# A hybrid delta-rule and pooling layer: the chunk inverse in 16-bit pairs, and the order of the work around it

## The chip, the cores and the metric

The kernel runs on one core of a Trainium2 chip, in one launch. A core has a matrix engine (TensorE, PE in the profile; its weight loads are PEld), three engines for elementwise work (VectorE is DVE, ScalarE is ACT, GpSimd is POOL) and SyncE (SP), which here issues the DMAs. The metric is the device time of one execution in microseconds; times of kernels are medians of several runs.

## The reference

One layer over 2048 new frames of one stream and 64 of a running one, model width 1024, all in float32. A norm and one combined input projection feed two groups: a gated delta rule (4 heads of 128, evaluated in chunks) and a pooling group (four trailing means with a linear map each). Both go through one output projection; then follow a norm, a SwiGLU layer of inner width 2816 and a last norm. The part that matters here is the chunk's inverse T of a unit lower triangular matrix:

```python
q, k, v = causal_conv_silu(...)               # q, k l2-normalised per head
G = cumsum(g)                                 # log decay, per head and chunk
gamma = exp(where(lower_incl, G[:, None] - G[None, :], -inf))
Lm = where(lower_strict, (k * beta) @ k.T * gamma, 0)
T = inverse(eye + Lm)                         # unit lower triangular
u, w = T @ (v * beta), T @ (k * beta * exp(G))
for each chunk, with the state S:
    v_new = u - w @ S
    o = (q * exp(G)) @ S + ((q @ k.T) * gamma) @ v_new
    S = S * exp(G_last) + (k * exp(G_last - G)).T @ v_new
x = x + concat(rmsnorm(o) * silu(z), pool) @ w_out
h = rmsnorm(x)
x = x + (silu(h @ w_gate) * (h @ w_up)) @ w_down
```

The kernel takes chunks of 128 frames rather than the reference's 64, which gives the same result. The projection, a product with the state and the outputs stay in float32 or in pairs that carry about its precision.

## The kernel before

**Two phases.** The first (to about 985 us in the profile) goes through four blocks of 512 frames, the first with the 64 frames of the running stream besides. A block has a norm (`norm_stats`, `norm_apply`), 21 projection tiles of 128 columns (`project`, products `pp`): one for the gates, four for each head (`head_project`) and four for pooling (`pools`), and later eight tiles of output projection (`out_proj`, products `pz`). The second phase goes over three blocks of 704 frames: 22 gate and up tiles (`gate_up`, products `px`, `py`, `pz`), and the down projection in six groups of inner tiles.

**Dense products.** Every float32 operand of a dense product is split into a high and a low half of a reduced format (`split`, `wsplit`), and three products stand for one; these are the type "r" of the scheduler. Gate, up and most down groups use Strassen's scheme (7 products instead of 8, `down_strassen`, `factors`, `prep_down`); the groups listed in `PLAIN` are done without it (`down`, products `d`).

**The inverse.** Each head of each block has two `Front`s of two chunks each, 32 in all, and the running stream has one. A front makes the decay matrix (gb: the row of G by `rowmm`, minus G by `negmm` with `seln`, a mask by `idbf` with `negm`, then one exponential into Gam), the matrix U (Gst) and then its inverse by doubling, in six steps after a first one: POOL masks U (Um), PE multiplies (py), ACT evicts to f16 (Yt), PE multiplies (pt), DVE updates T and its transpose V, all 2 x 2 x 128 columns (TV). The last step writes float32; then two corrections in full float32 (type "f" of the scheduler, two records each in the profile) take away the error of f16: F = 1 - T - U T (pf), and X = V + F (V + F V) (two products px), each evicted by DVE. Behind the inverse a chain goes through the chunks (pk, po, Sp).

**What sets the order.** No engine is programmed by hand: `Machine` records all operations and issues each engine's in an order that a list scheduler gives, from estimated costs (`Machine.cost`; for DVE 0.15 + 1.045e-3 x elements, in us) and a rank, the place in the program minus `machine.boost`. Chains of the inverse are boosted by `BOOST`. On PE, f16 and float32 products go ahead of dense ones, once the last of them has been ready for `HOLD[0]` us or so (`Machine.pick`). The order is then fixed, and semaphores keep what is needed.

**Buffers that matter.** PSUM tiles of the dense products come from a ring of `PSM` = 3 (pc, the product of the decay rows Rt, takes one of these). `evict` empties a projection; in block 0 it is DVE that does so, and multiplies by the norm's factor rn. `bp` holds h, as two tiles of four of the eight 128-row parts each (h0 and h1), one buffer each. `new_o(last_prev, bp, None, 1)` puts the operand op of block 2's output projection into those same buffers, when block 3 has projected; `out_proj` uses op's second tile (op1, parts 4 to 7) first. The loads for it (od) go through a ring of three (xc). In the second phase the loads of h (`load_h`, xh and xhT) go through f2's ring "t" of seven from its start on, which the gates' evictions use as well.

Of the kernel before, what the change touches and what calls it, by code (L numbers as in the profile page):

```python
# [9 lines left out]
F16 = mybir.dt.float16  # L10
# [8 lines left out]
P = 128  # L19
D = 1024  # L20
# [27 lines left out]
PLAIN = ((0, 0), (0, 1), (0, 2), (0, 3), (0, 5), (1, 2), (2, 2))  # L48
# [10 lines left out]
class Machine:  # L59
# [294 lines left out]
def hybrid_kernel(ctx, tc, a, o):  # L354
# [131 lines left out]
    for j in range(NBLK):  # L486
# [4 lines left out]
        else:  # L491
            plan += win[:9] + win[17:] + win[9:17]
# [40 lines left out]
    def prep():  # L533
# [8 lines left out]
        elif key[0] in ("win", "wout"):  # L542
            parts = []
            for i in range(2):
                raw, t = (f() for f in wtiles(f"p{i}"))
                src = a[key[0]][key[1]][:, 512 * i : 512 * i + 512]
                nc.sync.dma_start(out=raw, in_=wpd[key[1]] if key[0] == "wout" and i else src)
                if key == ("win", 0):

                    r3, h3, l3 = (x.rearrange("p (k c) -> p k c", c=P) for x in (raw, t[:, 0], t[:, 1]))  # L550
                    nc.gpsimd.memset(l3[:, :, 64:].bitcast(F32), 0.0)
                    nc.scalar.copy(l3[:, :, :64], r3[:, :, :64])
                    nc.scalar.copy(h3[:, :, :64], r3[:, :, :64])
                    tt(h3[:, :, 64:], r3[:, :, 64:], l3[:, :, :64].bitcast(F32), ALU.subtract)
                else:
                    wsplit(t, raw)
# [197 lines left out]
    def norm_apply(B):  # L754
# [62 lines left out]
    nc.sync.dma_start(out=consts, in_=a["consts"])  # L817
# [22 lines left out]
    lm_f = gp.tile([P, 2, 512], F32, tag="Yqk", name="lm_f", bufs=NY).rearrange("p i (l n) -> p (i l) n", n=P)  # L840
    nc.sync.dma_start(out=lm_f, in_=a["lmask"])
    lmask = cp1.tile([P, 7, P], F16, tag="lmask", name="lmask")
    nc.vector.tensor_copy(lmask, lm_f[:, :7])
    negm = cp1.tile([P, P], BF16, tag="negm", name="negm")
    nc.vector.tensor_copy(negm, lm_f[:, 7])

    negm2 = cp1.tile([P, P], BF16, tag="negm2", name="negm2")
    nc.vector.tensor_copy(negm2, lm_f[:, 7])
    nc.vector.memset(negm2[:DEC, DEC:], -1e30)
    id16 = cp1.tile([P, P], F16, tag="id16", name="id16")  # L850
    nc.vector.tensor_copy(id16, ident)
    idbf = cp1.tile([P, P], BF16, tag="idbf", name="idbf")
    nc.vector.tensor_copy(idbf, ident)

# [5 lines left out]
    nc.vector.memset(Sp, 0.0)  # L860

# [6 lines left out]
    class Front:  # L868
# [39 lines left out]
        def negmm(self, ps):  # L908

            G = self.B.Ghl  # L910
            if self.h is None:
                for h in range(NH):
                    mm(ps[:, h * DEC : (h + 1) * DEC], G[:, SO : SO + P], seln[:, h, :].to_broadcast([P, DEC]),
                       start=False, stop=False)
            else:
                for c in range(2):
                    at = self.off + c * C
                    mm(ps[:, c * C : (c + 1) * C], G[:, at : at + C], seln[:, self.h, :].to_broadcast([P, C]),
                       start=False, stop=c == 1, skip_group_check=True)

        def all(self):
# [22 lines left out]
            TV32 = lev(F32, "TV32", "", [P, 2, 2, C])  # L944
            gb = self.ps(f"gb_{tag}")
            self.rowmm(gb, True)
            EG = TV32[:, 0]
# [6 lines left out]
            dd = gb if self.h is not None else self.ps(f"dd_{tag}")  # L954
# [832 lines left out]
```

## Time and profile before

| | |
|---|---|
| median of 3 runs | 2384.84 us (2381.84 to 2387.46) |
| profiled execution, its own time | 2383.12 us |
| its span | 2380.5 us |
| mean granted TensorE clock | 0.997 |
| two record forms of the inverse, py and pt in f16 | 448 and 768 records |
| DMA moved over the span | 540.57 MB |

The span reaches from the first to the last instruction; 2.6 us lie around it. Nearly all instructions carry line 278, that of the recorder, so groups are told apart by their tiles: `pp<-h,wsp` is a projection, `px<-hA,ws` a gate product, `pz` an output projection where it reads op and a gate product where it reads hB. `_p` marks the heads of the prompt, `_s` the running stream. A row of a group gives its operations, their busy time and the mean ns of one, and behind the second bar the engine's idle time ahead of them with what ended it.

### The profile page before, as it was taken

The page shows a single profiled execution, that of the slowest core. Times are in us where ns is not written, and L with a number is a line of the kernel's source. Part 1 is how long each engine was busy: PE and PEld are TensorE (multiplying, and loading weights), DVE is VectorE, ACT ScalarE, POOL GpSimd, SP SyncE. Part 2 cuts the span into 40 slices and gives each one's busy share as a digit, 9 for nine tenths or more (in the row PEclk, how much of TensorE's full clock was granted, in tenths as well). Part 3 has the DMA queues.
Part 4 walks back from the last instruction along what each step waited for, and adds up shares of the span by engine and source line. Part 5 has one row for each costly group of instructions (what it writes and reads, how often), then busy time and mean ns, then how long its engine had stood idle before and what let it go on. Part 6 is the DMA issues. An engine that isn't in the chain of part 4 may idle for free.

```text
span 2380.5 us, 41651 instructions
## 1 busy us (share of the span) xinstructions
PE 2344.3 (98%) x14823; PEld 2184.7 (92%) x14823; DVE 1674.3 (70%) x2943; ACT 1215.7 (51%) x2738; POOL 967.2 (41%) x1130
## 2 busy tenths in 40 slices
PE   9999999999999999999999999999999999999998
PEld 8999798777887778899999999999999999999998
DVE  7999875785577686787776883767566657646466
ACT  6666654564456565574454654553334554425334
POOL 1656452554346662264332536353233464202211
PEclk9999999999999999999999999999999999999999
DMA  7643566445555565998876678887855697565763
GB/s 267 224 165 134 189 228 217 146 165 190 176 182 172 162 195 166 311 373 324 312 282 240 257 270 271 295 287 248 283 189 175 201 348 247 193 227 193 260 209 114
DMA packets 228384, 540.57 MB, mean 227 GB/s; under 512 B 28240, under 2 KB 86608, under 8 KB 228176
## 3 DMA queue, kind: packets, MB, share of 16 engines
q1 hardware_dynamic: 228176, 537.92, 66.2%
q8 instruction: 116, 1.90, 0.3%
q14 instruction: 92, 0.75, 0.1%
HBM read 389.41 MB, written 148.41 MB: 226 GB/s over the span
## 4 chain that ended last, share of the span: by engine, by line
PE 81%; DVE 9%; ACT 3%; DMA 3%; issue 2%; SPq 1%; POOL 1%; DVEq 0%; POOLq 0%; ACTq 0%
PE px L278 19%; PE pp L278 14%; PE pz L278 11%; PE py L278 9%; PE d L278 8%; PE dx L278 5%; PE dy L278 3%; PE pk_p L278 2%; PE pt_p L278 1%; PE dz L278 1%; PE gr_p L278 1%; PE px_p L278 1%; DVE Yqk L278 1%; PE py_p L278 1%; ACT E L278 1%
## 5 line engine op out<-in xcount | busy, mean ns | idle before, releaser
L278 PE MATMUL pp<-h,wsp 128*128 128x512 f32 (+1 forms) x2480 | 562.1, 366 | 2.0 <-DVE h L278 1.7
L278 PEld LDWEIGHTS pp<-h,wsp 128*128 128x128 f32 x2480 | 402.3, 190 | 49.8 <-DVE h L278 2.6
L278 POOL TENSOR_TENSOR Um_p<-Gst_p,lmask 128x256 f16<-128x256 f32 x224 | 178.2, 809 | 109.6 <-PE py_p L278 80.9
L278 PE MATMUL pz<-op,wsp 128*128 128x512 f32 (+1 forms) x960 | 216.8, 366 | 3.4 <-ACT op L278 2.9
L278 PE MATMUL d<-h3l,wsd 128*128 128x352 f32 x1248 | 201.3, 322 | 0.2 <-DVE h3l L278 0.2
L278 PEld LDWEIGHTS d<-h3l,wsd 128*128 128x128 f32 x1248 | 199.1, 188 | 1.2 <-DVE h3l L278 0.7
L278 PEld LDWEIGHTS pz<-op,wsp 128*128 128x128 f32 x960 | 155.9, 190 | 23.2 <-ACT op L278 3.4
L278 DVE TENSOR_TENSOR TV_p<-TV_p,pt_p 128x512 f16<-128x512 f16 (+1 forms) x192 | 128.5, 681 | 48.7 <-PE pt_p L278 43.4
L278 PE MATMUL px<-hA,ws 128*128 128x352 f32 x792 | 141.2, 322 | 0.6 <-DMA ws<-g 0.6
L278 PE MATMUL pz<-hB,ws 128*128 128x352 f32 x792 | 139.6, 322 | 0.6 <-DMA ws<-g 0.6
L278 PE MATMUL px<-hBT,ws 128*128 128x352 f32 x792 | 137.8, 322 | 2.1 <-DVE u L278 2.1
L278 PE MATMUL px<-hBT,wsS 128*128 128x352 f32 x792 | 137.7, 322 | 2.0 <-ACT g L278 1.9
L278 PE MATMUL py<-hB,wsS 128*128 128x352 f32 x792 | 139.2, 322 | 0.1
L278 PE MATMUL px<-hA,wsS 128*128 128x352 f32 x792 | 137.4, 322 | 0.9 <-ACT g L278 0.9
L278 PE MATMUL py<-hA,wsS 128*128 128x352 f32 x792 | 137.1, 322 | 0.0
L278 ACT ACTIVATE hr<-g 128x352 f32<-128x352 f32 x132 | 65.6, 497 | 133.4 <-DVE g L278 133.4
L278 PEld LDWEIGHTS px<-hBT,wsS 128*128 128x128 f32 x792 | 128.2, 188 | 2.8 <-ACT g L278 2.8
L278 PEld LDWEIGHTS px<-hBT,ws 128*128 128x128 f32 x792 | 128.0, 188 | 2.9 <-DVE u L278 2.7
L278 PEld LDWEIGHTS px<-hA,ws 128*128 128x128 f32 x792 | 128.9, 188 | 1.0 <-DMA ws<-g 0.9
L278 PEld LDWEIGHTS pz<-hB,ws 128*128 128x128 f32 x792 | 128.6, 188 | 0.8 <-ACT hB L278 0.8
L278 PEld LDWEIGHTS px<-hA,wsS 128*128 128x128 f32 x792 | 128.3, 188 | 1.2 <-ACT g L278 1.1
L278 PEld LDWEIGHTS py<-hB,wsS 128*128 128x128 f32 x792 | 128.6, 188 | 0.4 <-ACT u L278 0.4
(686 smaller groups left out, 5354.5 us busy)
## 6 DMA issues: line engine op xcount, KB each, us to landing
wsS<-gS SPq DMA_DIRECT2D x176, 512.0 KB, 4.7
ws<-g SPq DMA_DIRECT2D x132, 512.0 KB, 4.6
wsp<-wnd SPq DMA_DIRECT2D x126, 512.0 KB, 3.3
gS<-wsS SPq DMA_DIRECT2D x88, 512.0 KB, 5.6
g<-ws SPq DMA_DIRECT2D x66, 512.0 KB, 5.5
wnd<-wsp SPq DMA_DIRECT2D x42, 512.0 KB, 4.5
xd<-x2d SPq DMA_DIRECT2D x96, 176.0 KB, 4.0
wrd<-in_wd_dram SPq DMA_DIRECT2D x48, 256.0 KB, 4.7
```

The source lines that it names most:

```text
L278: getattr(getattr(self.nc, op.eng), name)(*args, **kw)
```

## The change

- `Front.all`: the inverse stays in f16 to its end. The update of a step writes only the half of T and V that the step can alter (`fresh`, an access pattern of runs of 2, 4, ... 64 elements), in place. U is kept as a pair of f16 halves scaled by `FS` = 256 (Uhl), and so is F (Fhl). F0 = 1 - T comes from POOL in f16, pf takes four f16 products, and the two px become one accumulation: Fhl's high half with V (evicted as FV), then its low half with V, T with 256 x identity, and Fhl's high half with FV.
- The decay matrix: `negmm` goes for the heads of the prompt; each chunk's exponential takes minus G as a bias (NG, one more small activation in `rows`).
- `Machine.pick` prefers, among the f16 and float32 products that are ready, the kind that was issued last; `HOLD[0]` is 0.6 instead of 0.4.
- `PLAIN` loses (0, 3): that down group uses Strassen's scheme now.
- The last block's pool tiles stand behind its four heads, not behind two, with h0 and h1 swapped in `new_o`.
- `norm_apply` from block 1 on: POOL multiplies by the norm's factor, ACT applies the weight as it splits, DVE makes the low half.
- `evict` ranks its operation ahead by `HURRY` = 400.
- The start: the gates' weights come in one load of 256 KB instead of two, and the first head's weights are prepared halfway through `norm_apply`; 104 of the 1384 columns of constants come early, the others and the masks behind `rows`; 19 products warm PE up instead of 22.
- `load_h` uses wpool's ring "xs" of four in all cases.

```diff
-PLAIN = ((0, 0), (0, 1), (0, 2), (0, 3), (0, 5), (1, 2), (2, 2))
+PLAIN = ((0, 0), (0, 1), (0, 2), (0, 5), (1, 2), (2, 2))
...
-            first = others[0]
+            first = min(others, key=lambda x: ((x[2].kind == "f") != (self.last == "f"), x))
...
-            plan += win[:9] + win[17:] + win[9:17]
+            plan += win
...
                     t = src(k, lo, n)
-                    stt(t, t, w, B.r[:, sl], ALU.mult, ALU.mult)
-                    split(h, sl, t)
-                if B.j == lo == 0 and k == 3:
+                    nc.gpsimd.tensor_tensor(out=t, in0=t, in1=B.r[:, sl], op=ALU.mult)
+                    act(h[:, 0, sl], t, AF.Copy, scale=w)
+                    stt(h[:, 1, sl], t, w, h[:, 0, sl].bitcast(F32), ALU.mult, ALU.subtract)
+                if B.j == lo == 0 and k % 4 == 3:
...
     def evict(B, dst, pp, p, b, n):
 
+        was, machine.boost = machine.boost, HURRY
...
+        machine.boost = was
...
-    nc.sync.dma_start(out=consts, in_=a["consts"])
+    nc.sync.dma_start(out=consts[:, :SOON], in_=a["consts"][:, :SOON])
...
+    def fresh(t, s):
+
+        (row, n), _ = t.ap
+        return bass.AP(t.tensor, t.offset, [[row, n], [2 * C + s, 2], [2 * s, 2 * C // (2 * s)], [1, s]])
...
+                mm(gb[:, : 2 * C], idbf, bc(negm, 2, C), start=False, stop=True, skip_group_check=True)
+                for c in range(2):
+                    act(Gam[:, c], two(gb)[:, c], AF.Exp, bias=self.B.NG[:, self.c0 + c, self.h : self.h + 1])
...
-                    tt(new, TV, pt.rearrange("p (t c n) -> p t c n", t=2, n=C), ALU.subtract)
-                TV = new
+                    new = fresh(TV.rearrange("p t c n -> p (t c n)"), 1 << l)
+                    tt(new, new, fresh(pt, 1 << l), ALU.subtract)
+                if l == 2:
+                    Uhl = lev(F16, "Uhl", "", [P, 2, 2, C])
+                    act(Uhl[:, 0], U, AF.Copy, scale=FS)
+                    stt(Uhl[:, 1], U, FS, Uhl[:, 0], ALU.mult, ALU.subtract)
...
-                mm(pf[:, c * C : (c + 1) * C], U[:, c], T[:, c], start=True, stop=True)
-            tt(F, F, two(pf), ALU.subtract)
+                for i in range(2):
+                    mm(pf[:, c * C : (c + 1) * C], Uhl[:, i, c], T[:, c], start=i == 0, stop=i == 1)
+            F = lev(F32, "F")
+            stt(F, F0, FS, two(pf), ALU.mult, ALU.subtract)
+            Fhl = lev(F16, "Fhl", "", [P, 2, 2, C])
+            nc.scalar.copy(Fhl[:, 0], F)
+            tt(Fhl[:, 1], F, Fhl[:, 0], ALU.subtract)
...
-                mm(px[:, c * C : (c + 1) * C], F[:, c], V[:, c], start=True, stop=True)
-            tt(T, V, two(px), ALU.add)
+                mm(px[:, c * C : (c + 1) * C], Fhl[:, 0, c], V[:, c], start=c == 0, stop=True, skip_group_check=c > 0)
+            FV = lev(F16, "Yt", "g")
+            act(FV, two(px), AF.Copy, scale=1.0 / FS)
...
-                mm(px[:, c * C : (c + 1) * C], F[:, c], T[:, c], start=True, stop=True)
-            tt(X, V, two(px), ALU.add)
+                for i, (lhsT, rhs) in enumerate(((Fhl[:, 1, c], V[:, c]), (T[:, c], idfs), (Fhl[:, 0, c], FV[:, c]))):
+                    mm(px[:, c * C : (c + 1) * C], lhsT, rhs, start=False, stop=i == 2, skip_group_check=True)
+            act(X, two(px), AF.Copy, scale=1.0 / FS)
...
-        four = [(pool or opool).tile([P, 4, 2, MB], F32R, tag=tag or f"h{k}", name=f"op{k}_{B.j}", bufs=bufs) for k in range(2)]
+        four = [(pool or opool).tile([P, 4, 2, MB], F32R, tag=tag or f"h{1 - k}", name=f"op{k}_{B.j}", bufs=bufs) for k in range(2)]
...
-            if h == 1 and nxt is None:
+            if h == NH - 1 and nxt is None:
                 pools(B)
...
-                if "pool" in wq:
-                    raw = wq["pool"].tile([P, N2], F32, tag="t", name=f"xh{nm}{k}_{b}", bufs=TB)
-                else:
-                    raw = wpool.tile([P, 512], F32, tag="xs", name=f"xh{nm}{k}_{b}", bufs=XBUFS["xs"])[:, :N2]
+                raw = wpool.tile([P, 512], F32, tag="xs", name=f"xh{nm}{k}_{b}", bufs=XBUFS["xs"])[:, :N2]
...
-WARM = 22
+WARM = 19
...
-HOLD = 0.4, 3.0
+HOLD = 0.6, 3.0
```

Three places of the new order. The first is PE in block 0, where the first two inverses end; `p0_0_0` is block 0, head 0, front 0. Before, with pf and the two px as f32 products:

```order
L278 MATMUL pf_p0_0_0_364<-TV32_p0_0_0_218,Gst_p0_0_0_223 128x128 x2
L278 MATMUL pp0_8_288_257<-h1_0_105,wsp1_9_205 128x288
L278 MATMUL pp0_9_0_286<-h0_0_104,wsp0_10_210 128x288 x12
L278 MATMUL pp0_9_0_286<-h1_0_105,wsp1_10_212 128x288 x2
L278 MATMUL px0_p0_0_0_373<-TV32_p0_0_0_218,F_p0_0_0_363 128x128 x2
L278 MATMUL pf_p0_0_1_375<-TV32_p0_0_1_227,Gst_p0_0_1_232 128x128 x2
L278 MATMUL pp0_9_0_286<-h1_0_105,wsp1_10_212 128x288 x10
L278 MATMUL px1_p0_0_0_382<-TV32_p0_0_0_218,F_p0_0_0_363 128x128 x2
```

And now, on PE at the same inverse, the accumulation of one chunk (the other chunk's follows it):

```order
L278 LDWEIGHTS Fhl_p0_0_1_373
L278 MATMUL px_p0_0_1_377<-TV_p0_0_1_248,Fhl_p0_0_1_373 128x128
L278 LDWEIGHTS Fhl_p0_0_0_359
L278 MATMUL px_p0_0_0_368<-TV_p0_0_0_245,Fhl_p0_0_0_359 128x128
L278 LDWEIGHTS TV_p0_0_0_245
L278 MATMUL px_p0_0_0_368<-idfs_163,TV_p0_0_0_245 128x128
L278 LDWEIGHTS Fhl_p0_0_0_359
L278 MATMUL px_p0_0_0_368<-Ytg_p0_0_0_369,Fhl_p0_0_0_359 128x128
```

Four f32 products (px, of two chunks in two rounds) became eight in f16, two of them ahead for FV and three for each chunk.

The second place is DVE in block 0, where the projections' evictions (ext, the second tile's is `ext0_4`) and the decay rows (er, Rt, Ghl) meet. Before:

```order
L278 CAST Ghl0_157<-Rt0_161 32x643
L278 TENSOR_TENSOR wsp1_5_172<-wrp1_5_171,wsp1_5_172 128x512
L278 TENSOR_TENSOR Ghl0_157<-Rt0_161,Ghl0_157 32x643
L278 SCALAR_TENSOR_TENSOR Yqk0_0_166<-ext0_0_168,consts_96,Yqk0_0_166 128x512
L278 SCALAR_TENSOR_TENSOR st0_153<-ext0_0_168,consts_96,st0_153 128x64 x3
L278 TENSOR_TENSOR ext0_4_175<-pp0_2_0_180,rn0_110 128x288
L278 TENSOR_TENSOR ext0_4_175<-pp0_2_288_181,rn0_110 128x224
L278 TENSOR_TENSOR ext0_4_175<-pp0_2_288_181,rn0_110 128x64
```

On DVE now:

```order
L278 TENSOR_TENSOR ext0_0_169<-pp0_1_288_175,rn0_113 128x64
L278 TENSOR_TENSOR ext0_4_176<-pp0_2_0_181,rn0_113 128x288
L278 SCALAR_TENSOR_TENSOR er0_153<-xr0_152,er0_153 64x579
L278 SCALAR_TENSOR_TENSOR Yqk0_0_167<-ext0_0_169,consts_96,Yqk0_0_167 128x512
L278 TENSOR_SCALAR Rt0_154<-er0_153,coef_140 64x579
L278 TENSOR_TENSOR wsp0_5_171<-wrp0_5_170,wsp0_5_171 128x512
L278 SCALAR_TENSOR_TENSOR Rt0_154<-ones_97,Rt0_154 4x128 x4
```

The eviction of the second tile's first half moved from behind the decay rows and the convolution (st) to a place ahead of them.

The third place is PE at the end of block 3's projections, where block 2's output projection begins (`pz2_0_0`, reading op1). Before:

```order
L278 LDWEIGHTS Yt4_p3_2_1_2751
L278 MATMUL pt4_p3_2_1_2770<-TV13_p3_2_1_2735,Yt4_p3_2_1_2751 128x128
L278 MATMUL pp3_16_0_2661<-h1_3_2093,wsp1_100_2587 128x512
L278 MATMUL pz2_0_0_2710<-op1_2_2691,wsp1_101_2608 128x512
L278 LDWEIGHTS Um6_p3_2_0_2767
L278 MATMUL py6_p3_2_0_2768<-TV15_p3_2_0_2739,Um6_p3_2_0_2767 128x128
```

PE now, first the last product that reads h0 (whose buffer op1 takes), then the place where the projections end:

```order
L278 LDWEIGHTS Fhl_p3_2_1_2745
L278 MATMUL px_p3_2_1_2757<-Ytg_p3_2_1_2758,Fhl_p3_2_1_2745 128x128
L278 MATMUL pp3_20_0_2667<-h0_3_2045,wsp0_100_2597 128x512
L278 MATMUL pp3_19_0_2666<-h1_3_2046,wsp1_99_2575 128x512 x4
L278 LDWEIGHTS TV_p3_3_0_2693
```

```order
L278 MATMUL pk0_p3_2_1_2767<-vn0_p3_2_1_2772,ktl_p3_2_1_2563 128x128
L278 MATMUL po_p3_2__2682<-Gam_p3_2_1_2572,vn0_p3_2_1_2772 128x128
L278 MATMUL pp3_20_0_2667<-h1_3_2046,wsp1_100_2598 128x512 x2
L278 MATMUL pz2_0_0_2725<-op1_2_2706,wsp1_101_2623 128x512 x3
L278 LDWEIGHTS Um5_p3_3_0_2783
```

The last projections are the paired pool tiles 19 and 20 instead of the last head's tile 16: all 24 products with h1 stand between h0's last reader and the output projection.

More of the change, by code (lines that the diff above doesn't have):

```diff
@@ L910, in negmm @@
             G = self.B.Ghl
[L911 to L914, printed above, removed]
-            else:
[L916 to L919, printed above, removed]
+            for h in range(NH):
+                mm(ps[:, h * DEC : (h + 1) * DEC], G[:, SO : SO + P], seln[:, h, :].to_broadcast([P, DEC]),
+                   start=False, stop=False)
         def all(self):
@@ L953, in all @@
             tt(Qd, self.Yqk[:, 0, self.off : self.off + 2 * C].rearrange("p (c n) -> p c n", n=C), EG, ALU.mult)
[L954 to L961 removed]
+            Gam = self.QKG = gt([P, 2, C], F32, "Gam", NOUT)
+            if self.h is None:
+                dd = self.ps(f"dd_{tag}")
+                mm(dd[:, : 2 * C], idbf, bc(negm2, 2, C), start=True, stop=False)
+                self.negmm(dd)
+                self.rowmm(dd, False)
+                act(Gam, two(dd), AF.Exp)
+            else:
+                mm(gb[:, : 2 * C], idbf, bc(negm, 2, C), start=False, stop=True, skip_group_check=True)
+                for c in range(2):
+                    act(Gam[:, c], two(gb)[:, c], AF.Exp, bias=self.B.NG[:, self.c0 + c, self.h : self.h + 1])
             U = lev(F32, "Gst")
@@ L981, in all @@
                 nc.gpsimd.tensor_tensor(out=Um, in0=U, in1=bc(lmask[:, l], 2, C), op=ALU.mult)
-                new = TV32 if l == nlev - 1 else lev(F16, f"TV{l % 2}", l, [P, 2, 2, C])
                 py = self.ps(f"py{l}_{tag}")
@@ L987, in all @@
                     idb = bc(id16, 2, C)
-                    tt(new[:, 0], idb, two(py), ALU.subtract)
-                    nc.gpsimd.tensor_tensor(out=new[:, 1], in0=idb, in1=Um, op=ALU.subtract)
+                    TV = lev(F16, "TV", "", [P, 2, 2, C])
+                    tt(TV[:, 0], idb, two(py), ALU.subtract)
+                    nc.gpsimd.tensor_tensor(out=TV[:, 1], in0=idb, in1=Um, op=ALU.subtract)
                 else:
```

85 lines of the change are left out of this document (45 added, 40 removed).

## The prediction

> **What bounds the kernel now.** I read the page first: busy times, then the chain that ended last.
>
> ```profile
> span 2380.5 us, 41651 instructions
> ...
> PE 2344.3 (98%) x14823; PEld 2184.7 (92%) x14823; DVE 1674.3 (70%) x2943; ACT 1215.7 (51%) x2738; POOL 967.2 (41%) x1130
> ...
> PE 81%; DVE 9%; ACT 3%; DMA 3%; issue 2%; SPq 1%; POOL 1%; DVEq 0%; POOLq 0%; ACTq 0%
> ```
>
> TensorE is busy for 98% of the span and idle for 2380.5 - 2344.3 = 36.2 us. So an edit is worth what it takes off TensorE's own stream, plus what it changes in those 36 us. Second, the waits of PE, to see what they are made of, and windows around the three longest, for the granted clock.
>
> ```profile
> PE pz L278 <- ACT op L278: 2.9, 2, 2.2
> PE pc L278 <- POOL ext L278: 2.9, 1, 2.9
> ...
> PE pk_p L278 <- DVE Sp L278: 1.7, 1, 1.7
> ...
> PE py_p L278 <- DVE TV_p L278: 0.7, 2, 0.5
> ```
>
> ```profile
> core 0: us, PE busy (x) PEld busy (x) DVE busy (x) ACT busy (x) POOL busy (x), PEclk, DMA share, GB/s
> 40.00:50.00 10.00, 7.92 (x50) 7.95 (x51) 7.88 (x20) 6.30 (x13) 0.74 (x5) 0.83 0.38 138
> 720.00:725.00 5.00, 3.47 (x17) 3.14 (x18) 4.89 (x10) 1.03 (x3) 1.28 (x3) 0.81 0.38 140
> 885.00:890.00 5.00, 3.84 (x9) 2.81 (x10) 3.86 (x7) 3.42 (x6) 1.78 (x2) 0.69 0.87 306
> ```
>
> No wait repeats. The inverse's own (py_p on TV_p) cost 0.7 us in all: its chain is covered by dense products. The three longest each cost twice: after them the granted clock falls, by (1 - 0.83) x 10 = 1.7 us of work at 40-50 and (1 - 0.69) x 5 = 1.6 us at 885-890. [...]
>
> **The change part by part.** What one product costs is the distance from its start to the next start, since ends overlap. Third view: the timeline of PE.
>
> ```profile
> 707.61 0.61 PE L278 MATMUL px_p<-TV_p,F_p 128*128 128x128 f32 x4
> 707.97 0.71 PE L278 MATMUL pp<-h,wsp 128*128 128x512 f32 x2
> ...
> 874.63 0.39 PE L278 MATMUL pp<-h,wsp 128*128 128x512 f32 x1
> 874.86 0.28 PE L278 MATMUL pt_p<-Yt_p,TV_p 128*128 128x128 f16 x2
> 874.98 0.27 PE L278 MATMUL pt_p<-TV_p,Yt_p 128*128 128x128 f16 x2
> 875.09 0.28 PE L278 MATMUL pt_p<-Yt_p,TV_p 128*128 128x128 f16 x2
> 875.21 0.28 PE L278 MATMUL pt_p<-TV_p,Yt_p 128*128 128x128 f16 x2
> 875.29 0.48 PE L278 MATMUL pp<-h,wsp 128*128 128x512 f32 x1
> ```
>
> ```profile
> L278 PE MATMUL d<-h3l,wsd 128*128 128x352 f32 x1248 | 201.3, 322 | 0.2 <-DVE h3l L278 0.2
> ...
> L278 PE MATMUL px_p<-TV_p,F_p 128*128 128x128 f32 x256 | 40.6, 279 | 0.6 <-DVE TV_p L278 0.4
> ...
> L278 PE MATMUL pf_p<-TV_p,Gst_p 128*128 128x128 f32 x128 | 19.9, 277 | 0.0
> ...
> L278 PE MATMUL gb_p<-seln,Ghl 128*128 128x128 f32 x64 | 14.2, 306 | 0.0
> ...
> L278 PE MATMUL px_s<-TV_s,F_s 128*128 128x128 f32 x8 | 1.2, 274 | 0.0
> ...
> L278 PE MATMUL pf_s<-TV_s,Gst_s 128*128 128x128 f32 x4 | 0.6, 273 | 0.0
> ```
>
> A full-precision product of 128 columns leaves two records; four stand (0.61 - 0.279) / 3 = 0.11 us apart. Six f16 products take 875.21 - 874.86 = 0.35 us, 0.058 each. Six terms of TensorE's stream:
> - The inverses' last products in f32 go: 256 + 128 + 8 + 4 = 396 records x 0.11 = **-43.6**.
> - In their place each of the 33 inverses has twelve f16 products (four pf, eight px): 396 x 0.058 = **+23.0**.
> - The decay matrix's minus-G products (seln) go, 64. Bounds: 64 x 0.11 = 7.0, by the distance, and 14.2, the row's busy time with its tails; I take **-7.0**.
> - Down group (0, 3) turns from 8 x 2 x 12 = 192 products into 4 x 7 x 6 = 168: 24 x 201.3 / 1248 = **-3.9**.
> - Sorting by kind: the dense product after f16 lasts 0.48 instead of 0.39, 0.09 more, of which the two f16 products ahead (0.08 from 875.21 to 875.29, not 0.116) give back 0.03. So only leaving f16 costs (0.06). The order has 364 such exits before and 374 now: **+1**; a pass through f32 alone is nearly free, so sorting saves little.
> - Three of 22 warm-up products: 6 x 0.11 = 0.7 at most, nothing if the first operand comes late: **-0.4**.
>
> Their sum is -30.9. Now the waits, which the rest of the change moves. Fourth view: timelines of DVE, ACT and PE at the two waits that the order touches.
>
> ```profile
> 40.69 0.92 DVE L278 SCALAR_TENSOR_TENSOR st<-ext,consts,st 128x64 f32<-128x64 f32 x3
> 41.53 1.25 DVE L278 TENSOR_TENSOR ext<-pp,rn 128x288 f32<-128x288 f32 x4
> ...
> 885.49 1.92 ACT L278 CAST op<-od 128x512 fp32r<-128x512 f32 x3 [3.05 <-DMA od<-od]
> ...
> 886.16 4.08 PE L278 MATMUL pz<-op,wsp 128*128 128x512 f32 x9 [2.17 <-ACT op L278]
> ```
>
> - Evictions early. pc waits 2.9 us at 42 for a PSUM buffer that DVE's eviction of pp releases only at 41.5, behind the convolutions; in the new order the eviction stands ahead of the decay rows. That is -2.9 and the clock's -1.7. What is late next is Rt, which pc also needs. Bounds -4.6 and 0; I take **-3**. The smaller first loads and the later constants feed the same stretch and are in this term.
> - Pool tiles last. The op operand of block 2 lies where h of block 3 lay, so its loads and splits start when the last projection has read h; pz waits 2.9 us for them, and the clock takes 1.6. Now h's first half is read out some 24 products (24 x 0.23 = 5.5 us) earlier, and that half serves first. The loads still pass a ring of three. Bounds -4.5 and +1; I take **-3**.
>
> Fifth view: groups of the other engines, the nearest rows to what is new there.
>
> ```profile
> L278 DVE TENSOR_TENSOR TV_p<-TV_p,pt_p 128x512 f16<-128x512 f16 x160 | 107.2, 681 | 40.9 <-PE pt_p L278 35.9 <-POOL Gst_p L278 1.8 <-POOL TV_p L278 1.1
> ...
> L278 DVE SCALAR_TENSOR_TENSOR xb<-xb,nw,rn 128x512 f32<-128x512 f32 x24 | 24.2, 1036 | 0.9 <-ACT rn L278 0.9
> ...
> L278 DVE TENSOR_TENSOR X_p<-TV_p,px_p 128x256 f32<-128x256 f32 x32 | 13.3, 416 | 9.9 <-PE px_p L278 9.9
> ...
> L278 ACT CAST Yt_p<-py_p 128x256 f16<-128x256 f32 x192 | 68.4, 370 | 113.3 <-PE py_p L278 112.7
> ...
> L278 POOL TENSOR_TENSOR wrS<-wrS,wr 128x512 f32<-128x512 f32 x44 | 63.5, 1443 | 24.2 <-DMA wr<-in_wu_dram 17.9 <-DVE y L278 2.2 <-DVE wsS L278 1.2
> ```
>
> - Half updates: half of 512 elements. Bounds: 416 ns (256 elements, contiguous) and 681 ns (as before); nothing in the trace shows so short runs. I take 0.42, and **0** for the span either way, as DVE is covered.
> - The inverse's end has one hand-over more (F, its f16 half, px, FV, px, X), 0.37 us on ACT per row, and the two Gam activations, Uhl and X move onto ACT (51% busy), which has room. Dense products cover it: **0**. With no cover, 33 x (0.37 + about as much for hand-overs) = +24; half of that is the upper bound, +12.
> - The norm's first multiplication moves to POOL: 24 x 1.44 = 35 us on an engine idle for 59% of the span, in three bursts at the blocks' ends, while DVE loses one full pass of 1.04 and keeps one. **0**; bounds -3 (DVE is earlier there, as at 720) and +5 (the inverse's masks, on POOL too, are late).
> - Group (0, 3) and the h loads' ring:
>
> ```profile
> 1270.00:1310.00 40.00, 40.00 (x253) 40.00 (x253) 23.72 (x37) 11.64 (x21) 10.41 (x8) 1.00 0.47 177
> 1350.00:1400.00 50.00, 49.11 (x303) 48.11 (x302) 46.55 (x73) 24.84 (x50) 29.01 (x27) 1.00 0.54 196
> ...
> DMA to landing us min/median/max: 2.9/4.5/6.2
> ```
>
> The group runs plain at 1270-1310, with DVE at 59%; the Strassen group at 1350-1400 has DVE at 93% and PE loses 0.9 us. So **+1**, bounds 0 and 2. The h loads go to a ring of four that nothing else uses then, instead of seven buffers shared with the gates; four tiles now come far ahead, the others at 4 per 4.5 + 1.5 us (landing, two splits). **0**; bounds -2 and +4.
>
> Sum: -30.9 - 3 - 3 + 1 = **-35.9**. The profiled execution spans 2380.5 and took 2383.1 us, so 2347.2; it lies 1.7 us below the median shown, 2384.84, which gives 2349.
>
> **The rivals.**
> 1. The waits take work back: as the dense stream shrinks by 30 us, the inverse's longer end shows on PE, +12 in the sum: 2361. For it: the steps that move there stand in ACT's order behind casts and activations of the dense work. Against it: PE waited 0.7 us for TV_p in all, and ACT is idle for half the span.
> 2. Slower. The half update writes runs as short as two elements; if DVE steps slowly through them, all 6 x 33 = 198 updates are late, and PE's next product (py) stands in a fixed place.
>
> ```profile
> 708.79 0.67 DVE L278 TENSOR_TENSOR TV_p<-TV_p,pt_p 128x512 f16<-128x512 f16 x1
> ...
> 710.35 0.28 PE L278 MATMUL py_p<-TV_p,Um_p 128*128 128x128 f16 x2
> ```
>
> There the update ends at 709.46 and py starts 0.9 us later. With that slack behind the planned 0.42, an update begins to hold PE at 1.3 us; to eat 36 and add 5 it must take 1.3 + 41 / 198 = 1.5 us, over twice the 681 ns of the full one. Then 2390 and more. [...]
> 3. The orders don't free anything: pc waits for Rt and pz for its loads as long as before: -35.9 + 6 = 2355.
> 4. The waits go further than taken (both in full, -1.6 and -1.5, block ends -3, ring -2, group (0, 3) at no cost): 2349 - 9.1 = 2340.
>
> **How the numbers follow.** Forecast with rival 3, 2342 to 2356: 0.58. Rival 1, 2356 to 2370: 0.20. Rival 4: 0.13. Nearly all eaten, 2370 to 2390: 0.06, half of it within 0.2%. Slower: 0.03. A measurement here can tell about 0.2% (4.8 us) from no change. So faster 0.94, same 0.03, slower 0.03. The range, 2336 to 2366, is rival 4 with half of seln's upper bound besides (2340 - 3.6) at one end, and rival 1 with POOL's upper bound (+5) at the other.
>
> **What would show it.** PE records fall from 14823 by 94 to 14729, the px_p and pf_p groups turn f16 with starts 0.06 apart; PE busy falls by 25 to 31 us; pc's wait under 1.5 us and the granted clock 1.00 at 40-50; pz's wait on op under 1.5 us; TV_p's mean near 0.42. It is wrong if PE's idle time grows over 45 us, or if TV_p takes over 0.7 us and PE waits for it.

## The result, and the profile after

| | before | now |
|---|---|---|
| median of runs | 2385.63 us (4 runs) | 2343.24 us (4 runs, 2342.46 to 2348.24) |
| ratio, 95% interval | | 0.9834 [0.9822, 0.9846] |
| profiled execution, its span | 2380.5 us | 2346.5 us |
| mean granted clock | 0.997 | 0.995 |

The change saves 1.7% by the ratio, 42 us between the medians; the forecast was 36, from 2385 to 2349. The execution profiled first was the longest of the four; the same kernel in a second series took 2347.8 us at the median, 37 us less than before (ratio 0.9843 [0.9828, 0.9857]), with a profiled span of 2343.3. So a difference of 3 us between single executions means nothing here, and the two medians of one kernel lie 4.6 us apart.

First the page of the changed kernel: span, busy times and the shares of the chain that ended last.

```profile
span 2346.5 us, 41685 instructions
...
PE 2312.9 (99%) x14729; PEld 2143.9 (91%) x14729; DVE 1654.7 (71%) x2946; ACT 1269.6 (54%) x2920; POOL 1041.7 (44%) x1178
...
PE 83%; DVE 7%; DMA 4%; ACT 2%; issue 2%; POOL 0%; SPq 0%; DVEq 0%; POOLq 0%; ACTq 0%
```

PE's records fell by the 94 that were forecast and its busy time by 31.4 us; its idle time is 33.6 us, 2.6 less. In the totals the gain looks like stream alone. The waits of PE say that it isn't so simple:

```profile
PE px L278 <- ACT g L278: 7.0, 7, 1.5
PE px L278 <- DVE u L278: 3.7, 5, 1.1
PE pk_p L278 <- DVE rhs_p L278: 3.5, 2, 3.1
PE dy L278 <- DVE y L278: 2.0, 1, 2.0
...
PE pc L278 <- DVE Rt L278: 0.7, 1, 0.7
...
PE py_p L278 <- DVE TV_p L278: 0.2, 1, 0.2
```

The waits of pc on ext (2.9) and of pz on op (2.9) are gone, and with the first of them the clock's loss at 40 to 50 us. New are pk's 3.1 us at 697 and some 6 us of px in the second phase. Windows at the old places, and at the new one with what follows it:

```profile
core 0: us, PE busy (x) PEld busy (x) DVE busy (x) ACT busy (x) POOL busy (x), PEclk, DMA share, GB/s
40.00:50.00 10.00, 9.93 (x76) 9.96 (x77) 9.68 (x22) 6.88 (x17) 2.24 (x7) 1.00 0.56 206
695.00:700.00 5.00, 2.46 (x9) 1.75 (x9) 4.89 (x10) 0.71 (x2) 1.13 (x1) 0.77 0.52 156
700.00:705.00 5.00, 5.00 (x24) 4.30 (x23) 1.50 (x5) 2.52 (x6) 1.29 (x2) 0.55 0.00 0
885.00:890.00 5.00, 5.00 (x36) 3.83 (x35) 2.91 (x6) 1.68 (x4) 0.08 (x1) 1.00 0.61 202
```

The clock's loss behind pk's wait is (1 - 0.77) x 5 + (1 - 0.55) x 5 = 3.4 us, so this one place costs 6.5 us.

Groups of DVE: the half update costs what half of 512 elements was expected to cost, and the two low halves (Uhl, Fhl) are new work on DVE.

```profile
L278 DVE TENSOR_TENSOR TV_p<-TV_p,pt_p 128x256 f16<-128x256 f16 x192 | 77.1, 414 | 47.9 <-PE pt_p L278 45.3 <-POOL Um_p L278 0.8 <-POOL Gst_p L278 0.7
...
L278 DVE SCALAR_TENSOR_TENSOR Uhl_p<-Gst_p,Uhl_p 128x256 f16<-128x256 f32 x32 | 23.1, 726 | 0.2
...
L278 DVE TENSOR_TENSOR Fhl_p<-F_p,Fhl_p 128x256 f16<-128x256 f32 x32 | 19.2, 599 | 4.5 <-ACT Fhl_p L278 4.2
```

To tell stream from waits I price every product, in each kernel's order, at the median distance to the next start that products of its kind and width have between such neighbours in the trace of before. The sum is the **stream**; what is left of the time from the first to the last product is the **rest**: waits, the slower clock and small delays. Both are worked out from the traces; their size depends by a few us on how finely kinds are told apart. The change takes the stream from 2320.6 to 2290.5 (-30.1) and the rest from 50.2 to 46.3. By stages, in us, the rest in brackets (stages are cut at equal counts of projection and gate products):

| stage | before | now | now, second profile |
|---|---|---|---|
| first third of block 0's projections | 70.8 (10.4) | 63.0 (6.7) | 62.9 (6.6) |
| nearly to block 0's end | 148.4 (4.0) | 134.2 (3.8) | 134.2 (3.8) |
| to the middle of block 1 | 171.3 (5.0) | 179.4 (5.6) | 177.8 (4.0) |
| to the start of block 3 | 317.2 (1.5) | 305.8 (0.3) | 305.8 (0.4) |
| block 3's projections | 166.5 (7.5) | 173.8 (6.4) | 173.1 (5.7) |
| to the first gate product | 121.3 (6.9) | 100.2 (-0.5) | 100.2 (-0.5) |
| first twelfth of the gate and up products, with what lies between them | 76.8 (2.6) | 79.0 (4.8) | 80.7 (6.5) |
| second twelfth | 150.5 (-0.6) | 150.4 (-0.6) | 150.5 (-0.5) |
| third and fourth, group (0, 3) within | 240.3 (4.2) | 240.8 (8.5) | 241.5 (9.2) |
| the rest | 907.7 (8.8) | 910.1 (11.2) | 906.8 (8.0) |

The first phase gains 39 us and more, the second gives some back: group (0, 3) was to save 3.8 us of stream, and its stage is no shorter. In block 3's projections the place at 697 is the whole rest.

### The profile page after: what moved, and what is told of

It reads as the page before. It is cut to its first block, busy times and chain, and to the rows that moved or that the text cites. A ratio compares the mean times of both kernels' runs of the same rounds, so it can differ in the third digit from the quotient of the medians.

```text
span 2346.5 us, 41685 instructions
## 1 busy us (share of the span) xinstructions
PE 2312.9 (99%) x14729; PEld 2143.9 (91%) x14729; DVE 1654.7 (71%) x2946; ACT 1269.6 (54%) x2920; POOL 1041.7 (44%) x1178
## 4 chain that ended last, share of the span: by engine, by line
PE 83%; DVE 7%; DMA 4%; ACT 2%; issue 2%; POOL 0%; SPq 0%; DVEq 0%; POOLq 0%; ACTq 0%
PE px L278 18%; PE pp L278 17%; PE pz L278 11%; PE py L278 9%; PE d L278 7%; PE dx L278 7%; PE dy L278 3%; PE pk_p L278 2%; PE pt_p L278 2%; PE dz L278 2%; PE gr_p L278 1%; PE py_p L278 1%; DMA gS<-wsS 1%; DVE hq L278 1%; DVE y L278 1%
## 5 line engine op out<-in xcount | busy, mean ns | idle before, releaser
L278 PE MATMUL pp<-h,wsp 128*128 128x512 f32 (+1 forms) x2480 | 555.9, 365 | 1.7 <-DVE h L278 1.6
L278 POOL TENSOR_TENSOR Um_p<-Gst_p,lmask 128x256 f16<-128x256 f32 x224 | 190.1, 862 | 98.8 <-PE py_p L278 70.2
L278 PE MATMUL pz<-op,wsp 128*128 128x512 f32 (+1 forms) x960 | 207.5, 361 | 0.0
L278 PE MATMUL d<-h3l,wsd 128*128 128x352 f32 x1056 | 170.5, 322 | 0.2
L278 PEld LDWEIGHTS d<-h3l,wsd 128*128 128x128 f32 x1056 | 168.5, 188 | 1.0 <-DVE h3l L278 0.4
L278 PEld LDWEIGHTS py<-hA,wsS 128*128 128x128 f32 x792 | 128.5, 188 | 0.3 <-DVE wsS L278 0.3
```

The source lines that it names most:

```text
L278: getattr(getattr(self.nc, op.eng), name)(*args, **kw)
```

## The experiments

In each but e9 one part of the change is undone in the changed kernel, everything else as changed; the scheduler then orders all engines anew, so an experiment shows the part with what its order brings. Kernels of one series ran on the same chip: e1 to e4, e5 to e8, e9 to e12. The changed kernel itself is in the first of these alone (e1), and its two medians differ by 4.6 us, while those of before stay between 2383.7 and 2385.6. So for e5 to e12 a median within some 5 us of the changed kernel says little by itself, and the traces have to decide.

| run | median us | ratio to before, 95% | stream | rest |
|---|---|---|---|---|
| e1 as changed | 2347.80 | 0.9843 [0.9828, 0.9857] | 2290.5 | 43.2 |
| e2 inverse's end in f32 | 2357.55 | 0.9887 [0.9872, 0.9901] | 2311.4 | 34.4 |
| e3 whole updates | 2353.22 | 0.9871 [0.9856, 0.9885] | 2290.6 | 50.4 |
| e4 minus G on PE | 2353.43 | 0.9871 [0.9854, 0.9887] | 2296.4 | 43.9 |
| e5 pool tiles earlier | 2351.01 | 0.9858 [0.9845, 0.9872] | 2291.2 | 43.9 |
| e6 no HURRY at all | 2358.16 | 0.9890 [0.9877, 0.9904] | 2290.8 | 55.5 |
| e7 group (0, 3) plain | 2341.52 | 0.9818 [0.9805, 0.9832] | 2294.3 | 35.7 |
| e8 h loads in the ring of seven | 2344.75 | 0.9834 [0.9821, 0.9847] | 2290.5 | 41.4 |
| e9 before, f16 end alone | 2376.70 | 0.9962 [0.9949, 0.9974] | 2303.2 | 63.7 |
| e10 evictions by place | 2351.27 | 0.9854 [0.9841, 0.9868] | 2290.8 | 52.0 |
| e11 e7, and rows ranked lower | 2345.99 | 0.9833 [0.9819, 0.9846] | 2294.6 | 37.4 |
| e12 norm's product on DVE | 2347.42 | 0.9838 [0.9824, 0.9851] | 2291.1 | 47.1 |

**e1, the same kernel again.** No edit.

> The changed kernel as it is, once more. In the first comparison its four runs took 2342.5, 2342.7, 2343.8 and 2348.2 us, and the profiled one was the longest. Theory A (TensorE's stream plus waits that repeat): 2343 us median, ratio 0.982 to 0.984; a second profile has the 3.3 us wait of pk on rhs at 697 and the waits of px on the h operands at 962 to 1019 again, and nominal work of the stream 2290 us. Rival B (the waits of the second phase are an accident of one execution): a span near 2341 us, in which these waits, or the 2.1 us of dy on y at 1969, are gone.

Measured: 2347.8 us, span 2343.3. The waits of px at 962 to 1019 and pk's wait repeat; dy's 2.0 us on y at 1969 shrinks to 0.3. A holds for the waits, and B for that one; the median is 4.8 us over A's 2343.

**e2, the inverse's end.** Uhl goes, the last step writes float32 (TV32, over all columns), F is evicted as before, and (shortened)

```diff
-                for i in range(2):
-                    mm(pf[...], Uhl[:, i, c], T[:, c], start=i == 0, stop=i == 1)
+                mm(pf[...], U[:, c], T[:, c], start=True, stop=True)
...
-                for i, (lhsT, rhs) in enumerate(((Fhl[:, 1, c], V[:, c]), (T[:, c], idfs), (Fhl[:, 0, c], FV[:, c]))):
-                    mm(px[...], lhsT, rhs, start=False, stop=i == 2, skip_group_check=True)
-            act(X, two(px), AF.Copy, scale=1.0 / FS)
+                mm(px[...], F[:, c], T[:, c], start=True, stop=True)
+            tt(X, V, two(px), ALU.add)
```

> The changed kernel with the inverse's end in float32 as before (pf and the two px in f32, float32 last step), all else as changed. Theory A: 396 products of 0.11 us come and 396 of 0.058 go, about +21 us: 2364 us, PE busy 2334 us. Rival B (the f16 end's extra hand-over shows on PE as a wait, so that undoing it gives that back): +9 us, 2352. Rival C (the end in f16 also took waits away): over +25 us.

Measured: +9.8 us against e1. The stream grows by 20.9, as priced, but the rest falls by 9 to 12: pk's waits on rhs are gone from the list, and the rest around block 1's start falls from 4.0 to 0.9, in block 3's projections from 5.7 to 1.2. B's size; whether the longer end is the cause, or just another order, e2 alone doesn't say. Of what it gives back, 4.5 us and more lie in block 3's projections, where the wait at 697 is gone; but that wait is gone in e3, e5 and e12 too, which keep the f16 end, so this part goes with the order. Hence e9.

**e9, the other way round.** The kernel before with the new end of the inverse and nothing else: Uhl and Fhl, four pf, eight px, X and FV on ACT.

> The kernel before with the inverse's end in f16 alone (Uhl, Fhl, four pf, eight px; whole updates in two buffers, seln's products, the order's rules and all else as before). Undoing the same part in the changed kernel gave 10 to 14 us where the stream grew by 21. Theory A (waits follow the emitted order, not the inverse's end): -17 us, the emitted order's stream (396 x (0.11 - 0.058) = 20.6, less 3 for more exits from f16), 2367, give or take 5 by the order's other waits. Rival B (the longer end makes waits on PE): -5 to -9 us, 2376, and waits of py, px or pk of the inverse that the kernel before does not have.

Measured: -8.2 us (ratio 0.9962), of 17.4 us of stream, so 9.2 us are lost by the medians. In the profile, of an execution 2 us over its median, the rest grows by 13.5, 12.1 of it in the first two stages of the table (71.8 and 156.3 us with a rest of 11.6 and 14.9). Waits of PE in the whole of e9, most of them in block 0; the kernel before had 0.7 us of the first and none of the others:

```profile
PE py_p L278 <- DVE TV_p L278: 3.8, 7, 0.8
...
PE px_p L278 <- DVE Fhl_p L278: 0.9, 1, 0.9
...
PE pf_p L278 <- DVE TV_p L278: 0.6, 2, 0.4
```

One of them in the timeline of e9, DVE, POOL and PE:

```profile
97.55 1.85 DVE L278 SCALAR_TENSOR_TENSOR Yvz<-ext,consts,Yvz 128x512 f32<-128x512 f32 x1
97.57 1.28 POOL L278 TENSOR_TENSOR rn<-rn,sq7n 128x512 f32<-128x512 f32 x1
...
99.32 0.41 DVE L278 TENSOR_TENSOR Fhl_p<-F_p,Fhl_p 128x256 f16<-128x256 f32 x1
99.66 0.74 DVE L278 SCALAR_TENSOR_TENSOR Yvz<-ext,consts,Yvz 128x512 f32<-128x512 f32 x1
...
99.79 0.23 PE L278 MATMUL px_p<-TV_p,Fhl_p 128*128 128x128 f16 x1 [0.94 <-DVE Fhl_p L278]
99.86 0.22 PE L278 MATMUL px_p<-idfs,TV_p 128*128 128x128 f16 x1
99.91 0.22 PE L278 MATMUL px_p<-Ytg_p,Fhl_p 128*128 128x128 f16 x1
```

The accumulation itself is as cheap as priced, 0.05 to 0.07 us from start to start; it waits because F's low half stands on DVE behind a convolution of 1.85 us. That convolution runs beside a product of POOL; the next one, of the same size, takes 0.74. In this stretch DVE has little slack to give. Windows of before, of e9, of the changed kernel and of e2, for 60 to 230 us; behind the length of the window stand PE, PEld, DVE, ACT and POOL:

```profile
60.00:230.00 170.00, 167.97 (x1387) 156.34 (x1387) 161.77 (x327) 111.26 (x287) 106.06 (x154) 1.00 0.53 179
```

```profile
60.00:230.00 170.00, 163.51 (x1330) 148.20 (x1328) 159.30 (x312) 119.90 (x309) 97.21 (x144) 0.98 0.51 171
```

```profile
60.00:230.00 170.00, 167.46 (x1345) 151.32 (x1345) 154.41 (x324) 125.94 (x330) 114.29 (x155) 1.00 0.60 195
```

```profile
60.00:230.00 170.00, 169.11 (x1376) 155.21 (x1375) 150.94 (x329) 116.44 (x306) 117.55 (x161) 1.00 0.56 185
```

DVE is busy 95% there before, and 94% in e9, where it works through less of the program (1330 products of PE against 1387). Per inverse the f16 end takes two evictions of 0.42 off DVE and adds 0.73 and 0.60. In the stretch e9 waits some 5 us for operands of the inverse and of the chain behind it, where the kernel before waits 1.6, and its clock of 0.98 costs (1 - 0.98) x 170 = 3.4 us more. B holds: where DVE is full, the longer end is not covered.

DVE's 95% are not all work. In this window of before 54 of its records last at least 0.15 us longer than the shortest of the same tiles and shape, 23 us in sum; each of the 54 runs beside an operation of POOL for most of what it lasts longer. So part of DVE's load in block 0 goes with POOL's work; that POOL is its cause is not shown, as no run here varies it by itself.

**e3, whole updates.**

```diff
-                    new = fresh(TV.rearrange("p t c n -> p (t c n)"), 1 << l)
-                    tt(new, new, fresh(pt, 1 << l), ALU.subtract)
+                    tt(TV, TV, pt.rearrange("p (t c n) -> p t c n", t=2, n=C), ALU.subtract)
```

> The changed kernel with updates over all 512 columns, in place, instead of the strided half. Theory A (DVE is covered): within 2 us of the changed kernel, TV_p near 0.68 us instead of 0.41, DVE busy 50 us more. Rival B (the shorter update is part of the gain): +4 us or more, with more waits of py on TV_p, or, as DVE's other work comes later, of pk and px in the first phase.

Measured: +5.4 us against e1, at an unchanged stream; TV_p takes 0.68 again. The waits of its PE:

```profile
PE py_p L278 <- DVE TV_p L278: 3.4, 7, 1.0
...
PE pt_p L278 <- ACT Yt_p L278: 2.5, 1, 2.5
PE pf_p L278 <- DVE TV_p L278: 2.4, 2, 2.2
```

The first row is the update itself showing on PE (0.2 us in the changed kernel). The other two are order: Yt stands on ACT behind a square that waits 2.1 us for POOL, and the update of 835.4 behind a product on DVE whose load (xd) comes 4.2 us late. B holds in the time; some 3 us show as the update's own waits, the rest comes with the order. Half of the first row lies in block 0, but block 0's rest is as in e1: the loss is behind it, up to the middle of block 1, where the two waits at 223 and 310 us bring a halved clock as well (0.97 over 200 to 390 us, in the changed kernel 0.99 and 1.00).

**e4, minus G.** The 64 products of seln are back, and one exponential without a bias.

```diff
-                for c in range(2):
-                    act(Gam[:, c], two(gb)[:, c], AF.Exp, bias=self.B.NG[:, self.c0 + c, self.h : self.h + 1])
+                self.negmm(gb)
+                act(Gam, two(gb), AF.Exp)
```

> The changed kernel with the products of minus G (seln) back on PE and one exponential without a bias, instead of two with one. Theory A: 64 products come, +6 us by the distances of the starts in the emitted order, so 2349. Rival B (the products' busy time counts): +14 us, 2357. Rival C (the added activations had cost waits on ACT): under +3 us.

Measured: +5.6 us, stream +5.9, rest as in e1. A: the distance between starts is the price, not the busy time of the row.

**e5, the pool tiles.**

```diff
-            if h == NH - 1 and nxt is None:
+            if h == 1 and nxt is None:
                 pools(B)
...
-tag=tag or f"h{1 - k}"
+tag=tag or f"h{k}"
...
-                plan += win
+                plan += win[:9] + win[17:] + win[9:17]
```

> The changed kernel with the last block's pool tiles after its second head again, their weights in that order, and op in the buffers of h as before. Theory A (the prediction's term): the wait of pz on op returns with the halved clock behind it, +3 us, at most +4.5. Rival B (the stretch from the last projection to the first gate product, which lost 7.4 us of waits, owes them all to this part): +7 us. Rival C (these waits had gone through other parts): within 1 us.

Measured: 2351.0, 3.2 and 7.8 us above the two medians of the changed kernel. Block 3's projections and the stage behind them take 277.6 us instead of 274.0 and 273.3: +3.6 to 4.3. pz waits again:

```profile
PE pz L278 <- ACT op L278: 2.3, 2, 1.7
```

Windows of e5 around these waits, the granted clock third from the end:

```profile
840.00:860.00 20.00, 16.91 (x108) 12.30 (x107) 17.08 (x31) 12.97 (x28) 6.33 (x8) 1.00 0.82 194
860.00:890.00 30.00, 28.82 (x182) 22.16 (x181) 24.50 (x51) 19.27 (x58) 17.88 (x22) 1.00 0.71 223
```

The wait is A's, but the halved clock behind it doesn't return. The stretch to the first gate product alone has 7.3 us more of rest, as B said, 2 of it waits of pt and pk; the stretch ahead has 4 less, as pk's wait at 697 isn't there in this order. So the sum is A's, but it is made of two differences that A did not have.

**e6 and e10, the rank of evictions.** e6 sets HURRY to 0, by which the second phase's own evictions, which had this rank before the change too, lose it; e10 takes it from the projections' alone.

```diff
-        was, machine.boost = machine.boost, HURRY
+        was = machine.boost
```

> The changed kernel with evictions ranked by their place again (HURRY 0). Theory A: the wait of pc at 42 us returns, 2.9 us and 1.7 by the clock; +3 us, at most +4.6, all before 60 us. Rival B (the smaller first loads had taken that wait away): within 1 us before 60 us, and what else changes lies elsewhere in the first phase.

> The changed kernel with the projections' evictions ranked by their place; the rank of the second phase's own evictions, which the run before with HURRY 0 had taken away too, stays. Theory A (that run's slices: 7.2 us lost between 39 and 71 us, where pc waits 3.0 and the clock halves, and 5 in sum to the end of the first phase): +5 to +8 us, 2351. Theory B (the prediction's term): +3, at most +4.6. Rival C (the whole 13 us of that run belong to this rank): +12, 2357.

Measured: e6 2358.2, e10 2351.3. Both take 15 us longer in block 0 and 8 less in the stage behind it, as products move from one to the other; the first phase ends 7.9 us later in e10 than in the changed kernel's first profile, 10 later than in its second. The medians give +3.5 to +8. In e10:

```profile
40.00:50.00 10.00, 7.01 (x41) 6.81 (x40) 9.43 (x22) 6.64 (x15) 2.42 (x8) 0.80 0.66 231
50.00:60.00 10.00, 10.00 (x68) 10.00 (x67) 6.67 (x14) 5.74 (x11) 0.31 (x2) 0.86 0.23 75
60.00:100.00 40.00, 37.47 (x311) 35.12 (x310) 36.47 (x72) 28.35 (x81) 27.86 (x36) 1.00 0.64 220
```

```profile
PE pc L278 <- POOL consts L278: 3.0, 1, 3.0
...
PE py_p L278 <- DVE TV_p L278: 2.0, 4, 0.8
...
PE px_p L278 <- DVE Fhl_p L278: 1.3, 1, 1.3
```

pc's wait is back, 3.0 us, as A and B have it, but the clock behind it costs (1 - 0.80) x 10 + (1 - 0.86) x 10 = 3.4 us, where the kernel before lost 1.7: 6.4 us at this one place. The inverse's waits of e9 are back too, 3.3 us of py and px. Together that is about what the first phase loses, though the new order also loses the wait at 697 and has others. That early evictions let the dense products run on while DVE is full fits this, but no run separates it from the order. The time is A's. The other 7 us of e6 lie mostly in the second phase, where it is another edit.

**e7, group (0, 3).** `PLAIN` has (0, 3) again.

> The changed kernel with down group (0, 3) without Strassen's scheme again. Theory A (the prediction's terms): 24 products of 0.16 come, 1 us of waits goes, +3 us. Rival B (the slices of the trace: the stretch of that group takes 104.4 us in both kernels, as the waits of px on g and u there grew by 4.0 while the products shrank by 3.8): within 1 us, with the waits of px on g between 1195 and 1335 gone.

Measured: 2341.5, 2 to 6 us below the changed kernel; the intervals overlap. Windows of the same 145 us, the changed kernel and e7:

```profile
1158.00:1303.00 145.00, 140.50 (x869) 138.43 (x868) 124.03 (x189) 79.14 (x161) 73.48 (x59) 1.00 0.69 255
```

```profile
1158.00:1303.00 145.00, 143.30 (x899) 143.00 (x898) 111.28 (x167) 73.29 (x148) 48.67 (x35) 1.00 0.68 252
```

With Strassen PE issues 30 products fewer in this window and idles 4.5 us, as DVE rises from 111 to 124 and POOL from 49 to 73. B: the saved products and the waits cancel (the twelfth in which the group lies takes 104.4 and 104.9 us with it, 104.3 without), and the next one is 1.1 us longer for it.

**e8, the ring of the h loads.**

```diff
+                if "pool" in wq:
+                    raw = wq["pool"].tile([P, N2], F32, tag="t", name=f"xh{nm}{k}_{b}", bufs=TB)
```

> The changed kernel with the h loads of the second phase in the ring of seven again. Theory A (the prediction's term): 0, within 2 us. Rival B (the ring of four made the waits of px on the h operands between 962 and 1025, 4.8 us of waits in the first half of the gate products of block 0 against 2.6 before): -2 to -4 us there, and the 2.5 us of waits on h loads that the kernel before had at the third block's start return, so near 0 in sum but moved.

Measured: 2344.75, no difference. The rest of the first twelfth is 3.4 instead of 4.8 and 6.5, and a wait of px of 2.8 us stands at 1883. A in sum. B had the wrong releaser: the trace puts the waits at 962 to 1019, and the one at 1883, on g and u, the evictions of the gate products, not on a load.

**e11, the decay rows behind the chains.** e7's kernel, with

```diff
-        machine.boost = HOT_ROWS
+        machine.boost = HOT_ROWS if j == 0 else BOOST // 2
```

> The changed kernel with group (0, 3) plain again, and the decay rows of blocks 1 to 3 ranked at half of the chains' boost, so that DVE takes rhs ahead of the rows (Rt), not behind. Theory A (pk's wait on rhs near 697 us, 3.1 us, and the halved clock behind it come from the seven or eight decay-row operations that stand ahead of rhs on DVE): the wait goes, -3 to -4 us against the same kernel without that rank (2341.5), so 2338. Rival B (the rows are then late themselves): pc or gb waits for Rt or Ghl at the starts of blocks 1 to 3, and the time is 2341 to 2346.

This is aimed at the new wait at 697. DVE there, in the changed kernel and in e1:

```profile
690.43 4.50 DVE L278 TENSOR_TENSOR_SCAN Rt<-ones,Rt 4x128 f32<-4x128 f32 x4
694.95 1.84 DVE L278 TENSOR_SCALAR Rt<-Rt 4x128 f32<-4x128 f32 x4
696.81 0.41 DVE L278 CAST Ghl<-Rt 32x512 fp32r<-32x512 f32 x1
697.15 0.33 DVE L278 SCALAR_TENSOR_TENSOR rhs_p<-pk_p,EC,vtk_p 128x128 f32<-128x128 f32 x1
```

```profile
688.29 1.78 DVE L278 TENSOR_TENSOR_SCAN Rt<-ones,Rt 4x128 f32<-4x128 f32 x4
690.11 3.35 DVE L278 TENSOR_SCALAR Rt<-Rt 4x128 f32<-4x128 f32 x4
693.47 1.54 DVE L278 CAST Ghl<-Rt 32x512 fp32r<-32x512 f32 x1
694.93 0.33 DVE L278 SCALAR_TENSOR_TENSOR rhs_p<-pk_p,EC,vtk_p 128x128 f32<-128x128 f32 x1
```

Nine operations of the rows hold DVE for 6.7 us ahead of rhs; the scheduler's formula gives the eight short ones 0.28 us each, 2.3 in all. Measured for e11: pk's wait on rhs is gone from the list, but pc waits 1.7 us for Rt and gb 2.0 for ktl, and the median is 2346.0, 4.5 above e7 (another series; the intervals overlap). B: a wait moved, not removed.

**e12, the norm's product.** DVE multiplies again, and `split` as before.

> The changed kernel with the norm's first multiplication back on DVE and the split as before. Theory A (the prediction's term): 0, within 3 us. Rival B (POOL's 24 multiplications of about 1.4 us slow DVE or hold the inverse's masks): -3 to -5 us. Rival C (DVE's extra passes are late at the blocks' ends): +3 to +5 us, with pp waiting for h longer than 1.6 us in sum.

Measured: 2347.4, between the two medians of the changed kernel. A, within what the runs resolve; its waits stand elsewhere (none at 697, 3.4 us of py on TV_p at 822).

## Why the prediction came out right, point by point

- **The stream**, -30.9: measured -30.1. Single parts agree: the inverse's end 20.6 forecast and 20.9 in e2 (17.4 in e9, whose order leaves f16 more often), minus G 7.0 and 5.9 (e4), group (0, 3) 3.9 and 3.8 (e7).
- **"Dense products cover it: 0"**, of the inverse's longer end, is the step that failed. Put alone into the kernel before (e9) it loses 9 us by the medians and 13.5 in the profile, around the bound of 12 that the text took for half cover. That is rival 1's mechanism, with its size, though not rival 1's reason: the text looked at ACT's order, and the late operands come from DVE. It read the cover off py's 0.7 us of waits and ACT's idle half; DVE is busy for 162 of the 170 us from 60 to 230, a stretch of which the prediction shows no window. In the changed kernel the inverse's own waits (py, pt) are under 1 us; e2 gives 9 to 12 us back there, of which the place at 697 goes with the order, and how much of the others is the end's own stays open.
- **Half updates, 0, "as DVE is covered"**: failed too: DVE was not covered. The duration was right (0.42 taken, 0.414 measured); undoing it costs 5.4 us, some 3 of them as py's waits on TV_p, half of these in block 0.
- **Evictions, -3** (bounds -4.6 to 0): mis-sized. Undone (e10), the first phase ends 8 to 10 us later and the time rises by 3.5 to 8. The wait at 42 us was as told; the clock behind it cost 3.4 us, not 1.7, and the term had none of the 3.3 us by which the inverse then waits.
- **Pool tiles, -3**: 3.6 to 4.3 by the stages. The size is right; but it is 7.3 us behind the projections less 4 ahead, and in e5 the clock has no part in it.
- **Group (0, 3), -3.9 + 1**: the waits are 4.0 where 1 was taken, at most 2. The term is 0, or a small loss.
- **POOL's multiplication and the ring, 0 each**: right within what the runs resolve.
- The sorting, first loads, constants and warm-ups were not tried alone.

So the stream was forecast, and the rest came right in part by luck: the inverse's end gives about 10 us, not 20, and undoing the half updates and the evictions costs 5.4 and 3.5 to 8 us, where 0 and 3 were taken. One part loads DVE and two relieve it. That DVE's load in block 0 is what ties them together is shown for e9 alone; for the other two it is argued, as the orders differ too. What the signs of success in the prediction could show (records, busy time, pc, pz, TV_p's mean) all came true and none of them would have told this. Rival 2 fell: the updates take 0.414 us in the mean and 0.42 at most, and no run shows a cost of the short runs. What stays open besides: how much of e3's and e5's differences is the part and how much the order that comes with it; the rest varies between 36 and 56 us over orders whose streams lie within 6 us.

e7 is the fastest median measured, 1.7 us under the changed kernel's first and 6.3 under its second; it beats the kernel before clearly, the changed kernel not beyond doubt.

## What to carry to other kernels

When work is taken off a bound engine, its saving is certain only as far as its suppliers have slack in that very stretch: in e9, where DVE is busy for 159 of 170 us, 9.2 of 17.4 us were lost. Open the windows of every engine per stage before a hand-over is booked at nothing. Parts of a change that load and relieve the same engine don't add up one by one; one of them alone (e9) gave 8 us where the whole gave 40. A scheme with fewer products (Strassen's, in this one group) was worth nothing where an engine that prepares its operands rose from 111 to 124 of 145 us. And when single waits move with every new order, as the one at 697 does, undoing a part prices the part and the order together; a second experiment from the other side (e9 for e2) tells them apart in part.

## What the hardware showed unexpectedly

- Some short operations of DVE last longer beside POOL. The scan of 4 x 128 elements lasts 0.39 to 0.41 us in most records of the first two profiles and 0.63 to 1.44 us in the other ten, each of which runs beside POOL; six of the short ones do so too, for most of what they last. In e1 the four scans took 1.78 us, and the scalings behind them 3.35 instead of 1.84, at the time when POOL's products osq and pw run (689.8 to 693.4). The sum ahead of rhs is nearly the same, 6.7 and 6.6 us. Why some stretch and others don't, no run here shows.
- The updates in runs of 2 elements last as long as those in runs of 64, 0.41 us: means by run length in the trace of the changed kernel are 412 to 415 ns, all records within 397 to 423. The slow steps that rival 2 supposed don't show; other types were not tried.
- Waits of one length have different prices. pk's wait at 697 is 2.5 us in e1 and in e8. In e1 the granted clock falls behind it (0.83 over 690 to 700 and over 700 to 710, 3.4 us lost); in e8 it stays at 1.00 in both windows. In the traces of before and of the changed kernel, but for the start and the end of each, the clock stands at 0.50 for 3.4 us at a time (before from 43.8, 723.1 and 886.9 us on, now from 243.7, 1858.2 and 1970.9 on) and once for 6.8 us (now, from 697.7 on). So the waits were followed by a loss of 0 (e8), 1.7 (before, at 42 us) or 3.4 us (now and in e1, at 697).
